# Weight tiles with even and odd columns in separate halves, read one element in turn from each

## The chip, the core and the metric

The kernel runs on one core of one Trainium2 chip. The metric is the device time of one execution in microseconds; lower is better. A core has five engines that run side by side and meet at semaphores: TensorE (PE in the profile, with PEld for its loads of the stationary operand), VectorE (DVE), ScalarE (ACT), GpSimd (POOL) and SyncE (SP), which here issues the transfers of the weights from HBM. A matmul on TensorE holds a stationary operand of 128 x 128 and streams a moving operand of up to 512 columns past it; the result collects in PSUM.

## What is computed

One block of a hybrid layer, for 256 tokens and a model width of 4096, in float32. The parts that matter here are the large products with weights:

```python
h = _rmsnorm(x, norm_w[layer])
u = h @ w_in[layer]                  # 4096 x 15424 columns, split into 16 parts
...
y_ml = hm.reshape(B, S, ML_WIDTH) * jax.nn.sigmoid(ml_o) * jax.nn.silu(ml_z)
y_ns = _nsa(ns_q, ns_kc, ns_vc, ns_ks, ns_vs, ns_kw, ns_vw, ns_g, ...)
```

After these the two halves, the latter gated by silu(ns_z), are joined and multiplied by w_out (4096 x 4096), the input is added, and the sum goes through a last gate: a sigmoid of its product with ple_gate (4096 x 4096), times the product of p with ple_proj (256 x 4096), added to it. Between the products lie a chunked mLSTM, a compression of keys and values, and attention over 256 tokens; their own matmuls are small and have nothing to do with the change.

## The kernel before

**Precision.** Each float32 operand of a large product is held as two parts of the type fp32r, hi and lo, with hi + lo equal to the value up to rounding. A product of x and w is made of three matmuls: x_hi w_hi, x_lo w_hi, x_hi w_lo. The parts of the activations are the tiles sh and sl (and cb for sums and differences of blocks), 128 columns at a time as the stationary operand. The parts of the weights are the tiles whi and wlo; they are the moving operand.

**A unit of weights.** The weights are laid out on the host in blocks of 256 rows by 512 columns, or, for the groups with pairs, 128 rows by two blocks of 512 columns. Either way one unit is a tile of 128 partitions x 2 x 512 float32: 4096 bytes in each partition, the first block (j = 0) in the first 2048 and the second (j = 1) after it. `_blocks` makes this layout for w_in and ple_proj, `_pairs` for the gates, the early groups, w_out and ple_gate.

**The way of a unit.** `load` (L1391) issues its transfer on SP's queue into a raw tile, of which there are six; the first unit is loaded in two parts, one for each block (L1400). `split` (L1427) runs three units ahead of the product: ScalarE copies raw to whi, rounding it (L1416), and VectorE subtracts, wlo = raw - whi (L1417), both over the whole tile of 1024 elements a partition. There are four tiles of whi and of wlo. Then the unit's `mm` issues its matmuls, twelve of 512 columns for a full unit.

**Two kinds of groups.** In a wide group (`wide_group`, L869 and L871) sixteen units with 256 rows each are multiplied with both halves of the tokens. In a pair group (`pair_group`) a plan says, for each pair of row blocks kp, whether it is multiplied plainly ("C": `c_unit`) or by a scheme with seven products in place of eight ("a" and "c": `a_units`, `c_units`), which needs sums of weight blocks. Those sums are VectorE's, in place on raw tiles (`sums`, L1213 to L1217), and of one of its units only the second block is split (`split_one`, L1423 and L1424). Nearly all matmuls of pair groups are issued by `emit`, so their line is L1135 whatever called it; the last unit of the last group is issued in halves of 256 columns at L1248. The products with ple_proj are at L1310 to L1312.

**Order.** The order of the work is written out by hand: the loop at L1469 goes through the units, splits three ahead, issues the loads for which there is a free raw tile, and after each unit lets the smaller tasks (attention, mLSTM, evacuations) take a step.

**Other matmuls.** Units of kind "narrow" (L955, L956) use the split weights as the stationary operand, units of kind "raw" (L976) multiply with the raw tile; the change touches neither. VectorE's additions at L281 (compressed keys and values into xq, with steps of 120 elements in the output) and at L484 (biasc read in steps of 16 elements) are named in the prediction.

Of the kernel before, what the change touches and what calls it, by code (L numbers as in the profile page):

```python
# [13 lines left out]
AF = mybir.ActivationFunctionType  # L14
# [24 lines left out]
XN = (16, 19, 22, 25)  # L39
RAWB = 6  # L40
HALVES = slice(0, 256), slice(256, 512)

# [39 lines left out]
def hymba_block(ctx: ExitStack, tc: tile.TileContext, a, out: bass.AP):  # L84
    nc = tc.nc
# [764 lines left out]
    def wide_group(name, w, stat_flag, post, marks=None):  # L850

        flag = f"ev_{name}"
        box = {}
        prev = evq[-2] if len(evq) >= 2 else None
        evq.append(flag)

        def start():
            if prev:
                require(prev)
            box["ps"] = [psp.tile([128, 512], F32, tag=f"mm{t}", name=f"mm{t}", bufs=2) for t in range(2)]  # L860

        for u in range(16):
            def mm(hi, lo, u=u):
                for j in range(2):
                    c, k = divmod(2 * u + j, 4)
                    first, last = (u == 0 and j == 0), (u == 15 and j == 1)
                    for s, m, st in ((sh, hi, first), (sl, hi, False)):
                        for t in range(2):
                            MM(box["ps"][t], s[c][:, k, t * 128:(t + 1) * 128], m[:, j, :], start=st, stop=False)  # L869
                    for t in range(2):  # L870
                        MM(box["ps"][t], sh[c][:, k, t * 128:(t + 1) * 128], lo[:, j, :], start=False, stop=last)  # L871

            def pre(u=u):
                if u == 0:
                    start()
                if stat_flag and u % 2 == 0:
                    require(f"{stat_flag}{u // 2}")

            def fin(u=u):
                if marks and u % 2:  # L880
                    done.add(f"{marks}{u // 2}")
                if u == 15:
                    post(box["ps"], flag)

            gemm_unit(w[u], mm, pre, fin)
# [252 lines left out]
    def pair_group(g, w, stat):  # L1138
# [70 lines left out]
        def sums(kp, k):  # L1209

            r0, r = raw[kp]
            if k == 0:
                nc.vector.tensor_add(r0[:, 1], r0[:, 1], r0[:, 0])  # L1213
                nc.vector.tensor_add(r0[:, 0], r0[:, 0], r[:, 0])
            else:
                nc.vector.tensor_add(r[:, 0], r[:, 0], r0[:, 1])
                nc.vector.tensor_add(r[:, 1], r[:, 1], r[:, 0])  # L1217

        opened = deque()

# [7 lines left out]
        def c_unit(kp, k, last):  # L1228
            split = split_and_sum

            def mm(hi, lo):
                bl = blocks(kp)
                if last:

                    tail.append((bl, k, hi, lo))
                    if len(tail) < 4:
                        return
                    order = [(t, j) for j in range(2) for t in range(2)]
                    seq = [(b, i) for b in order[0:2] for i in range(3)] + [(b, 3) for b in order[0:2]]
                    for (t, j), i in seq + [(order[2], i) for i in range(4)]:  # L1240
                        bl, k_, hi, lo = tail[i]
                        emit(product(own[t][j], bl(k_, t), hi[:, j], lo[:, j]))
                    t, j = order[3]
                    for c in HALVES:
                        for i in range(4):
                            bl, k_, hi, lo = tail[i]
                            for s, m in ((0, hi), (1, hi), (0, lo)):
                                MM(own[t][j].t[:, c], bl(k_, t)[s], m[:, j, c], start=False, stop=i == 3 and m is lo and c is HALVES[1])  # L1248
                    return
                for j in range(2):  # L1250
                    both(*(product(own[t][j], bl(k, t), hi[:, j], lo[:, j]) for t in range(2)))

            def post():
                if k:
                    finish(kp)
            unit(w[kp, k], split, mm, kp, post=post)

        def a_units(kp):
            def split1(r):
                raw[kp] = [r]  # L1260
                return split_one(r)

            def split2(r):
                raw[kp].append(r)
                opened.extend(((kp, 0), (kp, 1)))
                return split_all(r, keep=True)

            def mm1(hi, lo):
                emit(product(oth[0], blocks(kp)(0, 0), hi[:, 0], lo[:, 0]))

            def mm2(hi, lo):
                both(product(own[0][0], mixed(kp, 2), hi[:, 0], lo[:, 0]),
                     product(own[0][1], blocks(kp)(1, 0), hi[:, 1], lo[:, 1]))
            unit(w[kp, 0], split1, mm1, kp, True)
            unit(w[kp, 1], split2, mm2, kp, True)

        def c_units(kp, last):
            def mm1(hi, lo):
                both(product(oth[3], mixed(kp, 1), hi[:, 0], lo[:, 0]),
                     product(oth[1], mixed(kp, 3), hi[:, 1], lo[:, 1]))  # L1280

            def mm2(hi, lo):
                both(product(oth[2], mixed(kp, 0), hi[:, 0], lo[:, 0]),
                     product(own[1][1], blocks(kp)(1, 1), hi[:, 1], lo[:, 1]))

            def post():
                finish(kp)
                if last:
                    urgent.append(t_x1_oth(g, oth) if 0 <= g < 4 else t_out_oth(g, oth, us))
                    if g in (-1, 3):  # L1290
                        new_activations(g, range(2), 0)
            unit(None, lambda _: split_and_sum(raw[kp][0], kp), mm1)
            unit(None, lambda _: split_and_sum(raw[kp][1], kp), mm2, post=post)

        def p_unit(j):
            box = {}

            def pre():
                require("p")
                require(f"own{g - 1}")  # L1300
                if g == 4:
                    require("r7")
                box["ps"] = [bank(1 - bset, 2 * j + t, [128, 512]) for t in range(2)]

            def mm(hi, lo):
                ps, ph, pl = box["ps"], held["ph"], held["pl"]
                for t in range(2):
                    tk = slice(t * 128, (t + 1) * 128)
                    for k in range(2):
                        MM(ps[t], ph[:, k, tk], hi[:, k, :], start=(k == 0), stop=False)  # L1310
                        MM(ps[t], pl[:, k, tk], hi[:, k, :], start=False, stop=False)
                        MM(ps[t], ph[:, k, tk], lo[:, k, :], start=False, stop=(k == 1))  # L1312

            def t_pj():
                if j == 0:
                    pj[0] = wk.tile([128, 2, 2, 512], F32, tag="a", name="pj")
                for t in range(2):
                    nc.scalar.activation(pj[0][:, j, t], box["ps"][t], AF.Copy)
                if j == 1:
                    done.add(f"pj{g}")  # L1320
                yield
            units.append(dict(src=a["ple_proj"][2 * (g - 4) + 1 - j], mm=mm, pre=pre, post=lambda: urgent.append(t_pj()),
                              kind="pair", split=lambda r: split_all(r)))
# [67 lines left out]
    def load(n):  # L1391
# [5 lines left out]
        raws[n] = wk.tile([128, 8, 64] if units[n]["kind"] == "narrow" else [128, 2, 512], F32, tag="raw", name="raw", bufs=RAWB)  # L1397
        if n == 0:
            for j in range(2):
                nc.sync.dma_start(raws[n][:, j], units[n]["src"][:, j])  # L1400
        else:
            nc.sync.dma_start(raws[n], units[n]["src"])
        if n in XN:
# [16 lines left out]

    def split_one(r):
        hi, lo = split_tiles()
        nc.scalar.activation(hi[:, 0], r[:, 1], AF.Copy)  # L1423
        nc.vector.tensor_sub(lo[:, 0], r[:, 1], hi[:, 0])  # L1424
        return hi, lo

    def split(n):  # L1427
        r = raws.pop(n, None)
        if n == 0:
            hi, lo = split_tiles()  # L1430
            for j in range(2):
                split_x(j)
                nc.scalar.activation(hi[:, j], r[:, j], AF.Copy)
                nc.vector.tensor_sub(lo[:, j], r[:, j], hi[:, j])
            splits[n] = (hi, lo)
            held_raw[0] -= 1
            return
# [69 lines left out]
def _blocks(w, cols):  # L1507

    k = w.shape[0]
    o = np.empty((len(cols), k // 256, 128, 2, 512), w.dtype)  # L1510
    for g, c in enumerate(cols):
        b = w[:, c:c + 512]
        o[g] = b.reshape(k // 256, 2, 128, 512).transpose(0, 2, 1, 3)
    return o


def _pairs(w):

    return np.ascontiguousarray(w.reshape(16, 2, 128, -1, 2, 512)[:, :, :, :, ::-1].transpose(3, 0, 1, 2, 4, 5))


def _layout(i):
# [50 lines left out]
```

## Time and profile before

| what | value |
|---|---|
| median of 3 runs | 2118.67 us (2118.36 to 2118.94) |
| span of the profiled execution, first to last instruction | 2116.5 us |
| what the median has over that span | 2.2 us |
| matmuls, all forms | 9696 |
| moved by the DMA engines | 422.08 MB, 199 GB/s on average |
| whole-tile splits, ScalarE L1416 | 839, mean 1060 ns |
| whole-tile splits, VectorE L1417 | 839, mean 1222 ns |

The time of the profiled execution by itself is not listed apart from the runs; its span is the time from its first to its last instruction. In the profile a row of a group has: line, engine, operation, output<-inputs by the program's names (for a matmul the moving operand comes first), the shape, the count, and after the bar the busy time in us, the mean duration of one in ns, and the idle time of the engine just before them with what ended it. A row of the timeline has the start in us, the duration in us, and the instruction. A row of windows has the stretch, its length, the busy time and count of PE, PEld, DVE, ACT and POOL, the granted clock of TensorE, the busy share of the DMA engines and GB/s. Records of matmuls overlap, since the next one starts while the last one's results are still on their way.

### The profile page before, as it was taken

What the parts mean: (1) busy time and instruction counts of PE and PEld (TensorE: products, weight loads), DVE (VectorE), ACT (ScalarE), POOL (GpSimd) and SP (SyncE); (2) the same over time, 40 slices, a digit from 0 to 9 for tenths busy, and PEclk for the clock granted to TensorE, in tenths of its full rate; (3) what the DMA queues carried; (4) which work ended last, traced back from release to release, by engine and by line L of the source; (5) the groups of instructions that cost most, each with busy time, mean ns of one, the idle gap of its engine ahead of it and who ended that gap; (6) DMA issues with size and microseconds to landing.
All of it is one profiled execution on the core that took longest, in us unless ns stands there. A gap on an engine that the chain in (4) does not pass through costs nothing.

```text
span 2116.5 us, 26925 instructions
## 1 busy us (share of the span) xinstructions
PE 2107.0 (100%) x9696; PEld 1739.3 (82%) x9696; DVE 1679.7 (79%) x2130; ACT 1198.6 (57%) x1545; POOL 30.3 (1%) x69
## 2 busy tenths in 40 slices
PE   9999999999999999999999999999999999999998
PEld 7888788888888888888888888888888888888887
DVE  6697588666656675859989999988898987888988
ACT  6656455555556555456555565666555555555554
POOL 1000000000000000000000000000000000000000
PEclk9999999999999999999999999999999999999999
DMA  9656866654455455646666667565666665666664
GB/s 354 211 185 206 285 203 216 195 167 159 145 174 159 151 177 168 196 145 200 200 206 209 192 207 229 182 213 180 224 211 216 229 221 169 204 201 224 203 218 145
DMA packets 118374, 422.08 MB, mean 199 GB/s; under 512 B 13714, under 2 KB 14026, under 8 KB 118240
## 3 DMA queue, kind: packets, MB, share of 16 engines
q1 hardware_dynamic: 115568, 413.45, 60.4%
q0 software_dynamic: 2528, 6.89, 1.1%
q8 instruction: 76, 1.25, 0.2%
q14 instruction: 58, 0.48, 0.1%
q10 hardware_dynamic: 144, 0.02, 0.0%
HBM read 416.08 MB, written 4.23 MB: 199 GB/s over the span
## 4 chain that ended last, share of the span: by engine, by line
PE 99%; DMA 0%; DVE 0%; ACT 0%; SPq 0%; issue 0%
PE mm L1135 34%; PE sd L1135 33%; PE mm L869 16%; PE mm L871 8%; PE sd L569 1%; PE sd L976 1%; PE sd L558 1%; PE sd L253 0%; PE sd L773 0%; PE sd L582 0%; PE sd L475 0%; DMA raw<-in_w_in 0%; PE sd L525 0%; PE sd L524 0%; PE sd L523 0%; PE mm L956 0%
## 5 line engine op out<-in xcount | busy, mean ns | idle before, releaser
L1416 ACT ACTIVATE whi<-raw 128x1024 fp32r<-128x1024 f32 x839 | 885.1, 1060 | 732.5 <-PE mm L869 133.8
L1417 DVE TENSOR_TENSOR wlo<-raw,whi 128x1024 fp32r<-128x1024 f32 x839 | 1021.9, 1222 | 343.1 <-ACT whi L1416 327.1
L1135 PE MATMUL sd<-whi,sh 128*128 128x512 f32 x852 | 276.1, 390 | 0.0
L1135 PE MATMUL sd<-wlo,sh 128*128 128x512 f32 x852 | 275.7, 389 | 0.0
L1135 PE MATMUL sd<-whi,sl 128*128 128x512 f32 x852 | 275.6, 389 | 0.0
L1135 PE MATMUL mm<-whi,sh 128*128 128x512 f32 x840 | 272.9, 393 | 0.3 <-ACT mv L200 0.3
L1135 PE MATMUL mm<-whi,sl 128*128 128x512 f32 x840 | 270.0, 389 | 0.0
L1135 PE MATMUL mm<-wlo,sh 128*128 128x512 f32 x840 | 269.9, 389 | 0.0
L869 PE MATMUL mm<-whi,sh 128*128 128x512 f32 x768 | 245.1, 400 | 1.4 <-ACT whi L1416 1.4
L869 PE MATMUL mm<-whi,sl 128*128 128x512 f32 x768 | 237.4, 390 | 0.0
L871 PE MATMUL mm<-wlo,sh 128*128 128x512 f32 x768 | 237.1, 390 | 0.0
L1135 PEld LDWEIGHTS sd<-wlo,sh 128*128 128x128 f32 x852 | 159.9, 188 | 33.2
L1135 PEld LDWEIGHTS sd<-whi,sl 128*128 128x128 f32 x852 | 159.9, 188 | 33.2
L1135 PEld LDWEIGHTS sd<-whi,sh 128*128 128x128 f32 x852 | 159.6, 188 | 33.3 <-issue 0.4
L1135 PEld LDWEIGHTS mm<-whi,sl 128*128 128x128 f32 x840 | 157.7, 188 | 33.1
L1135 PEld LDWEIGHTS mm<-wlo,sh 128*128 128x128 f32 x840 | 157.6, 188 | 33.1 <-DVE wlo L1417 0.2
L1135 PEld LDWEIGHTS mm<-whi,sh 128*128 128x128 f32 x840 | 155.8, 188 | 34.4 <-issue 2.7
L871 PEld LDWEIGHTS mm<-wlo,sh 128*128 128x128 f32 x768 | 144.0, 188 | 31.6 <-DVE wlo L1417 0.8
L869 PEld LDWEIGHTS mm<-whi,sl 128*128 128x128 f32 x768 | 144.2, 188 | 31.0
L869 PEld LDWEIGHTS mm<-whi,sh 128*128 128x128 f32 x768 | 139.6, 189 | 29.1 <-issue 1.9
L1135 PE MATMUL mm<-whi,cb 128*128 128x512 f32 x416 | 134.6, 389 | 0.0
L1135 PE MATMUL sd<-whi,cb 128*128 128x512 f32 x352 | 117.5, 389 | 0.0
(315 smaller groups left out, 1875.2 us busy)
## 6 DMA issues: line engine op xcount, KB each, us to landing
raw<-in_w_gate SPq DMA_DIRECT2D x192, 512.0 KB, 3.6
raw<-in_w_in SPq DMA_DIRECT2D x191, 512.0 KB, 3.5
raw<-in_w_out SPq DMA_DIRECT2D x128, 512.0 KB, 4.0
raw<-in_ple_gate SPq DMA_DIRECT2D x128, 512.0 KB, 3.5
raw<-in_w_early SPq DMA_DIRECT2D x96, 512.0 KB, 3.9
raw<-in_w SPq DMA_DIRECT2D x16, 512.0 KB, 4.3
u<-in_xt SPq DMA_DIRECT2D x16, 256.0 KB, 7.7
xn<-in_x SPq DMA_DIRECT2D x4, 1024.0 KB, 7.1
```

The costliest lines, as they stand in the source:

```text
L558: nc.tensor.transpose(psd[i][:, b, s, :], sb[i][:, b, s * 128:(s + 1) * 128], idn)
L569: MM(o[t][:, h, :], ptb[i][:, b, s, :], v[:, s, b, g * 128:(g + 1) * 128], start=False, stop=(i == 6 + t and b == 1 and s == t))
L869: MM(box["ps"][t], s[c][:, k, t * 128:(t + 1) * 128], m[:, j, :], start=st, stop=False)
L871: MM(box["ps"][t], sh[c][:, k, t * 128:(t + 1) * 128], lo[:, j, :], start=False, stop=last)
L976: MM(o[64 * kv:64 * kv + 60], xq[l // 8][:, l % 8, 60 * kv:60 * kv + 60], raw[:, j, 256 * kv:256 * kv + 256], start=(l == 0), stop=(l == 31))
L1135: MM(acc.t, s, m, start=acc.i == 0, stop=acc.i == acc.n - 1)
L1416: nc.scalar.activation(hi, r, AF.Copy)
L1417: nc.vector.tensor_sub(lo, r, hi)
```

## The change

The weights' layout and every access to it change together; the arithmetic is the same. The host now puts, for each partition, the even columns of both blocks into the first 2048 bytes and the odd columns into the second: in each half, 256 elements of block 0 and then 256 of block 1. Two helpers name the parts: `cols(m, j)` is block j as two runs of 256 elements, and `stream(m, j)` is block j in the order of its columns, with the half as the innermost index, so that successive columns are 512 elements apart, forth and back. Every matmul with whi or wlo as its moving operand uses `stream`; partial splits, the sums and the loads and splits of the first unit use `cols`. Whole-tile splits and loads stay as they are. Columns come out in PSUM in the order as before.

```diff
+def cols(m, j):
+    return m[:, :, 256 * j:256 * j + 256]
+
+def stream(m, j, c=slice(0, 512)):
+    return m[:, :, 256 * j + c.start // 2:256 * j + c.stop // 2].rearrange("p h b -> p b h")
...
-                            MM(box["ps"][t], s[c][:, k, t * 128:(t + 1) * 128], m[:, j, :], start=st, stop=False)
+                            MM(box["ps"][t], s[c][:, k, t * 128:(t + 1) * 128], stream(m, j), start=st, stop=False)
...
-                MM(box["ps"][t], sh[c][:, k, t * 128:(t + 1) * 128], lo[:, j, :], start=False, stop=last)
+                MM(box["ps"][t], sh[c][:, k, t * 128:(t + 1) * 128], stream(lo, j), start=False, stop=last)
...
-                nc.vector.tensor_add(r0[:, 1], r0[:, 1], r0[:, 0])
-                nc.vector.tensor_add(r0[:, 0], r0[:, 0], r[:, 0])
+                nc.vector.tensor_add(cols(r0, 1), cols(r0, 1), cols(r0, 0))
+                nc.vector.tensor_add(cols(r0, 0), cols(r0, 0), cols(r, 0))
...
-                    both(*(product(own[t][j], bl(k, t), hi[:, j], lo[:, j]) for t in range(2)))
+                    both(*(product(own[t][j], bl(k, t), stream(hi, j), stream(lo, j)) for t in range(2)))
...
-                nc.sync.dma_start(raws[n][:, j], units[n]["src"][:, j])
+                nc.sync.dma_start(cols(raws[n], j), cols(units[n]["src"], j))
...
-        nc.scalar.activation(hi[:, 0], r[:, 1], AF.Copy)
-        nc.vector.tensor_sub(lo[:, 0], r[:, 1], hi[:, 0])
+        nc.scalar.activation(cols(hi, 0), cols(r, 1), AF.Copy)
+        nc.vector.tensor_sub(cols(lo, 0), cols(r, 1), cols(hi, 0))
...
-        o[g] = b.reshape(k // 256, 2, 128, 512).transpose(0, 2, 1, 3)
+        o[g] = b.reshape(k // 256, 2, 128, 256, 2).transpose(0, 2, 4, 1, 3).reshape(k // 256, 128, 2, 512)
...
-    return np.ascontiguousarray(w.reshape(16, 2, 128, -1, 2, 512)[:, :, :, :, ::-1].transpose(3, 0, 1, 2, 4, 5))
+    v = w.reshape(16, 2, 128, -1, 2, 256, 2)[:, :, :, :, ::-1].transpose(3, 0, 1, 2, 6, 4, 5)
+    return np.ascontiguousarray(v).reshape(-1, 16, 2, 128, 2, 512)
```

The remaining hunks do the same to the other products of the pair groups, to the halves at L1248, to the products with ple_proj and to the split of the first unit.

More of the change, by code (lines that the diff above doesn't have):

```diff
@@ L1212, in sums @@
             if k == 0:
-                nc.vector.tensor_add(r0[:, 1], r0[:, 1], r0[:, 0])
-                nc.vector.tensor_add(r0[:, 0], r0[:, 0], r[:, 0])
-            else:
-                nc.vector.tensor_add(r[:, 0], r[:, 0], r0[:, 1])
-                nc.vector.tensor_add(r[:, 1], r[:, 1], r[:, 0])
+                nc.vector.tensor_add(cols(r0, 1), cols(r0, 1), cols(r0, 0))
+                nc.vector.tensor_add(cols(r0, 0), cols(r0, 0), cols(r, 0))
+            else:
+                nc.vector.tensor_add(cols(r, 0), cols(r, 0), cols(r0, 1))
+                nc.vector.tensor_add(cols(r, 1), cols(r, 1), cols(r, 0))
         opened = deque()
@@ L1241, in mm @@
                         bl, k_, hi, lo = tail[i]
-                        emit(product(own[t][j], bl(k_, t), hi[:, j], lo[:, j]))
+                        emit(product(own[t][j], bl(k_, t), stream(hi, j), stream(lo, j)))
                     t, j = order[3]
@@ L1247, in mm @@
                             for s, m in ((0, hi), (1, hi), (0, lo)):
-                                MM(own[t][j].t[:, c], bl(k_, t)[s], m[:, j, c], start=False, stop=i == 3 and m is lo and c is HALVES[1])
+                                MM(own[t][j].t[:, c], bl(k_, t)[s], stream(m, j, c), start=False, stop=i == 3 and m is lo and c is HALVES[1])
                     return
                 for j in range(2):
-                    both(*(product(own[t][j], bl(k, t), hi[:, j], lo[:, j]) for t in range(2)))
+                    both(*(product(own[t][j], bl(k, t), stream(hi, j), stream(lo, j)) for t in range(2)))
             def post():
@@ L1268, in mm1 @@
             def mm1(hi, lo):
-                emit(product(oth[0], blocks(kp)(0, 0), hi[:, 0], lo[:, 0]))
+                emit(product(oth[0], blocks(kp)(0, 0), stream(hi, 0), stream(lo, 0)))
             def mm2(hi, lo):
-                both(product(own[0][0], mixed(kp, 2), hi[:, 0], lo[:, 0]),
-                     product(own[0][1], blocks(kp)(1, 0), hi[:, 1], lo[:, 1]))
+                both(product(own[0][0], mixed(kp, 2), stream(hi, 0), stream(lo, 0)),
+                     product(own[0][1], blocks(kp)(1, 0), stream(hi, 1), stream(lo, 1)))
             unit(w[kp, 0], split1, mm1, kp, True)
@@ L1278, in mm1 @@
             def mm1(hi, lo):
-                both(product(oth[3], mixed(kp, 1), hi[:, 0], lo[:, 0]),
-                     product(oth[1], mixed(kp, 3), hi[:, 1], lo[:, 1]))
+                both(product(oth[3], mixed(kp, 1), stream(hi, 0), stream(lo, 0)),
+                     product(oth[1], mixed(kp, 3), stream(hi, 1), stream(lo, 1)))
             def mm2(hi, lo):
-                both(product(oth[2], mixed(kp, 0), hi[:, 0], lo[:, 0]),
-                     product(own[1][1], blocks(kp)(1, 1), hi[:, 1], lo[:, 1]))
+                both(product(oth[2], mixed(kp, 0), stream(hi, 0), stream(lo, 0)),
+                     product(own[1][1], blocks(kp)(1, 1), stream(hi, 1), stream(lo, 1)))
             def post():
@@ L1309, in mm @@
                     for k in range(2):
-                        MM(ps[t], ph[:, k, tk], hi[:, k, :], start=(k == 0), stop=False)
-                        MM(ps[t], pl[:, k, tk], hi[:, k, :], start=False, stop=False)
-                        MM(ps[t], ph[:, k, tk], lo[:, k, :], start=False, stop=(k == 1))
+                        MM(ps[t], ph[:, k, tk], stream(hi, k), start=(k == 0), stop=False)
+                        MM(ps[t], pl[:, k, tk], stream(hi, k), start=False, stop=False)
+                        MM(ps[t], ph[:, k, tk], stream(lo, k), start=False, stop=(k == 1))
             def t_pj():
@@ L1432, in split @@
                 split_x(j)
-                nc.scalar.activation(hi[:, j], r[:, j], AF.Copy)
-                nc.vector.tensor_sub(lo[:, j], r[:, j], hi[:, j])
+                nc.scalar.activation(cols(hi, j), cols(r, j), AF.Copy)
+                nc.vector.tensor_sub(cols(lo, j), cols(r, j), cols(hi, j))
             splits[n] = (hi, lo)
```

## The prediction

> **What bounds the kernel now.** I read the page's busy shares first, then the chain that ended last, then the groups of instructions with their shapes kept apart, and last the timeline of TensorE near the end.
>
> ```profile
> span 2116.5 us, 26925 instructions
> ...
> PE 2107.0 (100%) x9696; PEld 1739.3 (82%) x9696; DVE 1679.7 (79%) x2130; ACT 1198.6 (57%) x1545; POOL 30.3 (1%) x69
> ...
> PEclk9999999999999999999999999999999999999999
> ...
> PE 99%; DMA 0%; DVE 0%; ACT 0%; SPq 0%; issue 0%
> PE mm L1135 34%; PE sd L1135 33%; PE mm L869 16%; PE mm L871 8%; PE sd L569 1%; PE sd L976 1%; PE sd L558 1%; PE sd L253 0%; PE sd L773 0%; PE sd L582 0%; PE sd L475 0%; DMA raw<-in_w_in 0%; PE sd L525 0%; PE sd L524 0%; PE sd L523 0%; PE mm L956 0%
> ```
>
> TensorE is at work in 2107.0 of 2116.5 us, at a granted clock in the top tenth throughout, and 99% of the chain that ends last is its own matmuls; the three lines L1135, L869 and L871 are 91% of it. Busy time alone wouldn't prove that TensorE is the limit, since a matmul's record covers more than the time it holds the next one back. So I look at the distance between starts, in the timeline of the last stage: the first and last of 36 matmuls of 512 columns, and the first and last of 24 of 256 columns.
>
> ```profile
> 2098.99 0.39 PE L1135 MATMUL sd<-whi,sh 128*128 128x512 f32 x1
> ...
> 2106.93 0.39 PE L1135 MATMUL sd<-wlo,sh 128*128 128x512 f32 x1
> 2107.15 0.28 PE L1248 MATMUL sd<-whi,sh 128*128 128x256 f32 x1
> ...
> 2109.90 0.28 PE L1248 MATMUL sd<-wlo,sh 128*128 128x256 f32 x1
> ```
>
> The 512-column ones start (2106.93 - 2098.99) / 35 = 0.2269 us apart, the others (2109.90 - 2107.15) / 23 = 0.1196 us. The difference is 107.3 ns for 256 columns: **0.419 ns for a column**, and 226.9 - 512 x 0.419 = 12 ns for a matmul besides. So 95% of a matmul's pace is the streaming of its moving operand, and the change alters just how that operand is read. Whatever it does to a column is paid in full: nothing covers it.
>
> **How many matmuls it touches.** In the groups of TensorE, the moving operand is the first name behind the arrow; every group with whi or wlo there is touched.
>
> ```profile
> L1135 PE MATMUL sd<-whi,sh 128*128 128x512 f32 x852 | 276.1, 390 | 0.0
> L1135 PE MATMUL sd<-wlo,sh 128*128 128x512 f32 x852 | 275.7, 389 | 0.0
> L1135 PE MATMUL sd<-whi,sl 128*128 128x512 f32 x852 | 275.6, 389 | 0.0
> L1135 PE MATMUL mm<-whi,sh 128*128 128x512 f32 x840 | 272.9, 393 | 0.3 <-ACT mv L200 0.3
> L1135 PE MATMUL mm<-whi,sl 128*128 128x512 f32 x840 | 270.0, 389 | 0.0
> L1135 PE MATMUL mm<-wlo,sh 128*128 128x512 f32 x840 | 269.9, 389 | 0.0
> L869 PE MATMUL mm<-whi,sh 128*128 128x512 f32 x768 | 245.1, 400 | 1.4 <-ACT whi L1416 1.4
> L869 PE MATMUL mm<-whi,sl 128*128 128x512 f32 x768 | 237.4, 390 | 0.0
> L871 PE MATMUL mm<-wlo,sh 128*128 128x512 f32 x768 | 237.1, 390 | 0.0
> L1135 PE MATMUL mm<-whi,cb 128*128 128x512 f32 x416 | 134.6, 389 | 0.0
> L1135 PE MATMUL sd<-whi,cb 128*128 128x512 f32 x352 | 117.5, 389 | 0.0
> L1135 PE MATMUL mm<-wlo,cb 128*128 128x512 f32 x208 | 72.0, 390 | 0.0
> L1135 PE MATMUL sd<-wlo,cb 128*128 128x512 f32 x176 | 62.3, 391 | 0.0
> ...
> L1310 PE MATMUL sd<-whi,ph 128*128 128x512 f32 x16 | 6.2, 389 | 0.0
> ...
> L1312 PE MATMUL mm<-wlo,ph 128*128 128x512 f32 x16 | 6.2, 389 | 0.0
> ...
> L1248 PE MATMUL sd<-whi,sl 128*128 128x256 f32 x8 | 2.3, 283 | 0.0
> ```
>
> L1135: 3 x 852 + 3 x 840 + 416 + 352 + 208 + 176 = 6228. L869 and L871: 3 x 768 = 2304. L1310 to L1312: six groups of 16 = 96. Together **8628 of 512 columns**, and 24 of 256 at L1248. They take 8628 x 0.2269 + 24 x 0.1196 = 1961 us, 93% of the span.
>
> **The price of a column read the new way.** Before, a matmul's 512 columns lie in one run of 2048 bytes. After, column 0 is read from the first half of the tile, column 1 from 2048 bytes further on, column 2 from beside column 0, and so on: no column lies beside the one read just before it. No matmul of this trace reads its moving operand so; all read runs (even the two-piece key tiles of L523 to L525 are runs of 128 or more). The nearest rows are VectorE's, where single elements are taken far apart.
>
> ```profile
> L1104 DVE TENSOR_TENSOR y<-y,u 128x1024 f32<-128x1024 f32 x8 | 9.7, 1218 | 0.0
> ...
> L1213 DVE TENSOR_TENSOR raw<-raw 128x512 f32<-128x512 f32 x96 | 65.7, 684 | 0.0
> ...
> L281 DVE TENSOR_TENSOR xq<-ct,pe_c 128x480 f32<-128x480 f32 x8 | 8.5, 1067 | 0.0
> ...
> L484 DVE TENSOR_TENSOR sc<-sd,biasc 128x60 f32<-128x60 f32 x8 | 1.7, 250 | 1.4 <-POOL sc L481 1.4
> ...
> L500 DVE TENSOR_TENSOR sc<-sc,mask_c 128x60 f32<-128x60 f32 x8 | 1.4, 219 | 0.1
> ```
>
> Over runs, VectorE pays (1218 - 684) / 512 = 1.04 ns for an element and 150 ns for the instruction. L281 writes each element 480 bytes from the one before and comes back beside an old one only after eight: (1067 - 150) / 480 = 1.91 ns, **1.83 times** the price of a run. L484 reads biasc in steps of 64 bytes and costs 250 ns where L500, as large and over runs, costs 219: 31 / 60 = 0.52 ns more for an element, **1.50 times**. That is one engine's write and one engine's read, at a pace slower than TensorE's, so they bound and don't settle the price. From below I can't exclude nothing at all: TensorE may hold both places open. From above there are two readings of the same rows. As a ratio they give TensorE 1.5 to 1.83 times a column's 0.419 ns. As a time in itself, if it is the memory and not the engine that sets it, they give 1.04 + 0.52 = 1.56 to 1.91 ns a column, about four times TensorE's present 0.419.
>
> I choose **twice 0.419 ns**. [...] A column then costs 0.419 ns more: 214.5 ns for a matmul of 512 columns, 107.3 for one of 256.
>
> [...]
>
> **The sum.** 8628 x 214.5 ns = 1850.7 us, 24 x 107.3 ns = 2.6 us: +1853 us. Against it stands a little idle time that slower matmuls fill: the 1.4 us at L869 waiting for whi at the start. The profiled span becomes 2116.5 + 1853 - 1.4 = 3968 us; the median of the runs is 2118.67, 2.2 us over that span, for what lies around it. **Forecast 3970 us.** The weight loads (PEld, 82%) run beside the matmuls and are not changed; a load has more time than before.
>
> **The other edits** cost nothing in this forecast. The full splits at L1416 and L1417 still run over the whole tile. The partial split (L1423, L1424) and the sums (L1213 to L1217) now go over two runs of 1024 bytes instead of one of 2048. They stand on VectorE, and what hides them is TensorE; where cover is thinnest is the mixed stage:
>
> ```profile
> 1005.70:1012.50 6.80, 6.80 (x32) 5.63 (x31) 6.69 (x8) 3.00 (x4) 0.00 (x0) 1.00 0.61 189
> ...
> L753 DVE TENSOR_TENSOR s<-s 128x256 f32<-128x256 f32 x13 | 5.5, 425 | 0.5
> ...
> L666 DVE TENSOR_TENSOR s<-mb,future_c 128x256 f32<-128x256 f32 x8 | 3.3, 416 | 0.0
> ```
>
> In that stretch TensorE is busy 6.80 and VectorE 6.69 of 6.80 us. At twice a column's time the same 30 matmuls take about 13.2 us and VectorE's 6.69 are covered twice over. If columns keep their price, the cover is 0.11 us. L753 (two runs) costs 9 ns more than L666 (as many elements), while L1104 shows two longer runs at the price of the plain slope; so 0 to 9 ns each, for 4 x 96 sums and 96 partial splits at most 480 x 9 ns = 4.3 us, if nothing hid it. The first weight load (L1400) keeps its two transfers and its bytes, in pieces half as long; it stands ahead of everything on SP's queue, and I bound its cost by 0 and the 3.5 us that a whole load takes to land.
>
> ```profile
> raw<-in_w_in SPq DMA_DIRECT2D x191, 512.0 KB, 3.5
> ```
>
> No wait is added, and no instruction or byte. What is late next in the forecast is still TensorE: at about 0.44 us a matmul the splits (1.06 and 1.22 us per tile of twelve matmuls) and the loads fall further behind the need for them.
>
> **The rivals.**
>
> *The columns keep their price* (the change then does nothing, whatever the order of the addresses): TensorE's reader fetches ahead and keeps both places open, so each fetch still serves several columns. For it: only two runs are interleaved here, against eight in L281, and the total of bytes touched is the same. Against it: both rows of VectorE show a penalty. Time: 2118.67 plus 0 to 4.3 + 3.5 us, 2119 to 2127, most likely 2119; this is the case that ends on the other side, not slower, and it decides at the point where two open runs are enough. [...] Chance 24%, of which 4% slower by over 0.2%.
>
> *A jump costs the memory's own time.* Each column pays 1.56 to 1.91 ns, as on VectorE. A matmul then takes 512 x 1.56 + 12 = 811 to 512 x 1.91 + 12 = 990 ns, 584 to 763 more: +5039 to +6583 us, 7.2 to 8.7 ms. For it: the penalty on VectorE is a time that no clock of TensorE need shorten. Against it: TensorE already fetches runs at 0.419 ns where VectorE needs 1.04, so its path is not VectorE's. Chance 18%.
>
> *A part of a step.* Some fetches overlap, as by the reading row's 1.50: 0.21 ns x 512 = 107 ns, +926 us, 3045 us; the case spans 2130 to 3600. Chance 10%.
>
> *The jump helps.* If the 12 ns beside the columns came from reads that collide with the writes of the next tile, alternating halves could remove up to 12 x 8652 ns = 104 us: 2015 us. Nothing shows that: the 12 ns are the same for both sizes above and hardly vary. Chance 2%.
>
> **How the numbers follow.** The forecast (a column twice as dear) has 46%, and its own range goes from 1.83 times a column (178 ns more, +1536, 3655 us) to a whole matmul doubled (226.9 ns more, +1958, 4077 us). 0.2% of this kernel, 4.2 us, is about what a measurement can tell. Faster: 2%. Within 0.2%: 24 - 4 = 20%. Slower: 46 + 18 + 10 + 4 = 78%. The range must reach from the unchanged case to the forecast's upper end to hold 24 + 10 + 46 = 80%; the fourfold case and the gain are left out: 2115 to 4080. It is wide since its two main cases lie far apart, with little between.
>
> **What would show it.** Right: in the changed profile the 512-column matmuls of L1135 and L869 start 0.44 us apart, L1248's 0.227; the untouched ones (L569, L523, L955) keep their durations; VectorE's and ScalarE's busy times stay near 1680 and 1199 us, at shares of some 42% and 30%; TensorE stays at 99% of the chain and at full granted clock. Wrong: starts 0.227 us apart (columns keep their price), 0.8 to 1.0 us (the memory's own time), or a lower granted clock, which no step here provides for. L1213 or L1424 longer by more than 9 ns would break the sentence on the other edits.

## The result: faster by 4%, where twice the time was forecast

The changed kernel takes 2035.29 us (median of 4 runs, 2032.81 to 2036.74) against 2118.6 us before (median of 4, 2118.36 to 2118.94). The ratio is 0.9605, with a 95% interval of 0.9592 to 0.9619. The forecast was 3970 us, with a range from 2115 to 4080: the sign was wrong, and the time lies below the range.

The page of the profile after, beside the lines shown of before (L1143 was L1135, L877 and L879 were L869 and L871, L1256 was L1248):

```profile
span 2032.8 us, 26925 instructions
...
PE 2014.3 (99%) x9696; PEld 1748.9 (86%) x9696; DVE 1671.9 (82%) x2130; ACT 1190.7 (59%) x1545; POOL 30.3 (1%) x69
...
PEclk9999999999999999999999999999999999999999
...
PE 90%; DVE 5%; ACT 3%; issue 2%; DMA 1%; SPq 0%; ACTq 0%; DVEq 0%
...
L1143 PE MATMUL sd<-whi,sh 128*128 128x512 f32 x852 | 267.2, 380 | 0.0
...
L1143 PE MATMUL mm<-wlo,sh 128*128 128x512 f32 x840 | 261.3, 379 | 0.9 <-DVE wlo L1425 0.5
...
L877 PE MATMUL mm<-whi,sl 128*128 128x512 f32 x768 | 228.4, 379 | 0.0
```

The same instructions, as many matmuls, the same clock; the touched matmuls of 512 columns last some 10 ns less, 379 in place of 389 in most groups. The timeline of the last stage, the same 36 and 24 matmuls as in the prediction:

```profile
2015.83 0.38 PE L1143 MATMUL sd<-whi,sh 128*128 128x512 f32 x1
...
2023.38 0.38 PE L1143 MATMUL sd<-wlo,sh 128*128 128x512 f32 x1
2023.60 0.27 PE L1256 MATMUL sd<-whi,sh 128*128 128x256 f32 x1
...
2026.17 0.28 PE L1256 MATMUL sd<-wlo,sh 128*128 128x256 f32 x1
```

Matmuls of 512 columns now start (2023.38 - 2015.83) / 35 = **215.7 ns** apart, against 226.9 before; those of 256 columns (2026.17 - 2023.60) / 23 = 111.7 ns, against 119.6. Taken for all of them, that gives 8628 x 11.2 + 24 x 7.9 ns = 96.8 us, an estimate of the gain. The span became 83.7 us shorter, so some 13 us were given back. Idle time of TensorE accounts for 9.0 of them (2116.5 - 2107.0 = 9.5 us before, 2032.8 - 2014.3 = 18.5 after); where the other 4 went was not followed. The chain shows the idle time too: TensorE's share fell from 99% to 90%, with 5% VectorE and 3% ScalarE. In the list of waits (who waited for whom: us in total, times, longest), these rows of TensorE are new:

```profile
PE sd L566 <- ACT s L549: 3.3, 6, 0.6
PE sd L1143 <- DVE wlo L1425: 2.8, 5, 0.9
PE mm L1143 <- DVE wlo L1425: 1.4, 3, 0.5
```

The list of before has no row of TensorE for either supplier. 3.3 us are waits in the attention, six between 470 and 719 us, for tiles that ScalarE writes; 4.2 us are waits for wlo, eight between 933 and 1570 us. In the mixed stage 30 matmuls took 6.80 us before, of which VectorE was busy 6.69; at 215.7 ns they want 6.47 us, which is less than VectorE needs. That does not make VectorE the limit of the whole stage. In this stretch of the changed kernel VectorE is as busy, 6.70 of 7.00 us, and TensorE is never idle:

```profile
1005.00:1012.00 7.00, 7.00 (x34) 6.14 (x33) 6.70 (x8) 3.77 (x5) 0.00 (x0) 1.00 0.71 213
```

A TensorE that is 5% faster (215.7 ns where it was 226.9) runs into its suppliers now and then, no more.

### The profile page after: what moved, and what is told of

The parts are those of the page before. It is cut to its first block, busy times and chain, and to the rows that moved or that the text cites. A ratio compares the mean times of both kernels' runs of the same rounds, so it can differ in the third digit from the quotient of the medians.

```text
span 2032.8 us, 26925 instructions
## 1 busy us (share of the span) xinstructions
PE 2014.3 (99%) x9696; PEld 1748.9 (86%) x9696; DVE 1671.9 (82%) x2130; ACT 1190.7 (59%) x1545; POOL 30.3 (1%) x69
## 3 DMA queue, kind: packets, MB, share of 16 engines
q8 instruction: 76, 1.25, 0.2%
## 4 chain that ended last, share of the span: by engine, by line
PE 90%; DVE 5%; ACT 3%; issue 2%; DMA 1%; SPq 0%; ACTq 0%; DVEq 0%
PE sd L1143 32%; PE mm L1143 32%; PE mm L877 13%; PE mm L879 7%; DVE wlo L1425 2%; ACT whi L1424 2%; ACT s L549 1%; DVE mx L544 1%; DVE s L542 1%; PE sd L984 1%; PE sd L781 1%; PE sd L261 1%; PE sd L577 0%; DMA raw<-in_w_in 0%; PE sd L483 0%
## 5 line engine op out<-in xcount | busy, mean ns | idle before, releaser
L1424 ACT ACTIVATE whi<-raw 128x1024 fp32r<-128x1024 f32 x839 | 879.0, 1055 | 660.1 <-DVE raw L1222 129.1
L1143 PE MATMUL sd<-whi,sh 128*128 128x512 f32 x852 | 267.2, 380 | 0.0
L1143 PE MATMUL sd<-whi,sl 128*128 128x512 f32 x852 | 266.8, 379 | 0.0
L1143 PE MATMUL sd<-wlo,sh 128*128 128x512 f32 x852 | 266.8, 379 | 0.0
L1143 PE MATMUL mm<-whi,sh 128*128 128x512 f32 x840 | 264.1, 383 | 0.6 <-ACT mv L208 0.3
L1143 PE MATMUL mm<-wlo,sh 128*128 128x512 f32 x840 | 261.3, 379 | 0.9 <-DVE wlo L1425 0.5
L1143 PE MATMUL mm<-whi,sl 128*128 128x512 f32 x840 | 261.0, 379 | 0.0
L877 PE MATMUL mm<-whi,sh 128*128 128x512 f32 x768 | 235.9, 389 | 1.6 <-ACT whi L1424 0.8
L879 PE MATMUL mm<-wlo,sh 128*128 128x512 f32 x768 | 228.6, 379 | 0.3
L877 PE MATMUL mm<-whi,sl 128*128 128x512 f32 x768 | 228.4, 379 | 0.0
L1143 PEld LDWEIGHTS sd<-whi,sl 128*128 128x128 f32 x852 | 161.0, 189 | 22.9
L1143 PEld LDWEIGHTS sd<-wlo,sh 128*128 128x128 f32 x852 | 161.0, 189 | 22.8
L1143 PEld LDWEIGHTS sd<-whi,sh 128*128 128x128 f32 x852 | 160.7, 189 | 23.0 <-ACT whi L1424 0.4
L1143 PEld LDWEIGHTS mm<-wlo,sh 128*128 128x128 f32 x840 | 158.4, 189 | 24.6 <-DVE wlo L1425 2.5
L1143 PEld LDWEIGHTS mm<-whi,sh 128*128 128x128 f32 x840 | 156.6, 189 | 25.9 <-issue 2.7
L1143 PEld LDWEIGHTS mm<-whi,sl 128*128 128x128 f32 x840 | 158.8, 189 | 22.5
L879 PEld LDWEIGHTS mm<-wlo,sh 128*128 128x128 f32 x768 | 145.0, 189 | 21.6 <-DVE wlo L1425 1.1
L877 PEld LDWEIGHTS mm<-whi,sl 128*128 128x128 f32 x768 | 145.1, 189 | 20.6
L877 PEld LDWEIGHTS mm<-whi,sh 128*128 128x128 f32 x768 | 140.1, 189 | 21.8 <-issue 1.9
L1143 PE MATMUL mm<-whi,cb 128*128 128x512 f32 x416 | 130.2, 379 | 0.0
L1143 PE MATMUL sd<-whi,cb 128*128 128x512 f32 x352 | 113.8, 379 | 0.0
```

Of the source, the lines that this page charges most:

```text
L877: MM(box["ps"][t], s[c][:, k, t * 128:(t + 1) * 128], stream(m, j), start=st, stop=False)
L879: MM(box["ps"][t], sh[c][:, k, t * 128:(t + 1) * 128], stream(lo, j), start=False, stop=last)
L1143: MM(acc.t, s, m, start=acc.i == 0, stop=acc.i == acc.n - 1)
L1424: nc.scalar.activation(hi, r, AF.Copy)
```

## The experiments

Two questions stood: what makes reading in turn quicker than a run (215.7 ns against 226.9), and what the 11 ns are that a run loses. Unless it is said otherwise, the kernels below are the change with another layout of a block and the matching order of reading; the sums, splits, loads and results are the same. Each was one run with a profile, beside one run of the kernel before (2118.5 to 2119.6 us). The pace is always that of the last 36 matmuls of 512 columns, as above, and two rows of the timeline show it.

**near_1024: in turn, but 1024 bytes apart.**

```diff
-    return m[:, :, 256 * j + c.start // 2:256 * j + c.stop // 2].rearrange("p h b -> p b h")
+    return m[:, j].rearrange("p (h b) -> p b h", h=2)[:, c.start // 2:c.stop // 2]
```

> Columns are read in turn from the two halves of their own block, 1024 bytes apart instead of 2048. Theory A (reading in turn from two places avoids what slows a run, wherever the places are): 512-column matmuls start 215.7 ns apart, time about 2035 us. Theory B (it is the two halves of the 4096-byte tile, a matter of where the places lie): 226.7 ns apart, about 2118 us.

```profile
2015.94 0.38 PE L1143 MATMUL sd<-whi,sh 128*128 128x512 f32 x1
...
2023.50 0.38 PE L1143 MATMUL sd<-wlo,sh 128*128 128x512 f32 x1
```

2034.67 us, 7.56 / 35 = 216.0 ns where the change has 215.7. The halves of the tile have no part in it (B falls).

**step2: no turns, every second place of a run.**

```diff
+    v = m[:, j].rearrange("p (b h) -> p h b", h=2)
+    return v if c.stop - c.start == 512 else v[:, c.start // 256]
```

> A block lies in one run; its even places are read first, then its odd ones, so that each element is 8 bytes from the one before and nothing is read in turn. Theory C (a run of neighbouring elements has a price of its own that any larger step avoids): 215.7 ns apart, about 2035 us. Theory A (only reading in turn helps): 226.7 ns apart, about 2118 us.

```profile
4023.11 0.63 PE L1144 MATMUL sd<-whi,sh 128*128 128x512 f32 x1
...
4038.90 0.63 PE L1144 MATMUL sd<-wlo,sh 128*128 128x512 f32 x1
```

4053.16 us and 451 ns: neither of the two that were expected. A step of 8 bytes costs what the prediction feared of 2048 bytes forth and back. So an order apart from neighbours can have a price (451 ns against 226.9), and the change, at 215.7, does not pay it.

**two_runs: a pattern with two dimensions, but runs.**

```diff
+    if c.stop - c.start == 256:
+        return m[:, c.start // 256, 256 * j:256 * j + 256]
+    return m[:, :, 256 * j:256 * j + 256]
```

> Columns 0 to 255 lie in the first half of the tile and 256 to 511 in the second; a product reads two runs of 256. Theory A and theory C: both see runs, so 226.7 ns apart or a little more for the second run, 2118 to 2130 us. Theory D (a pattern with two dimensions is handled otherwise than one with one): 215.7 ns, about 2035 us.

```profile
2100.85 0.39 PE L1145 MATMUL sd<-whi,sh 128*128 128x512 f32 x1
...
2108.79 0.39 PE L1145 MATMUL sd<-wlo,sh 128*128 128x512 f32 x1
```

2120.15 us, 226.9 ns: as before. The form of the pattern is nothing by itself (D falls).

**half_stat: half of the weight load, runs as before.** This is the kernel before with one line changed.

```diff
-            MM(acc.t, s, m, start=acc.i == 0, stop=acc.i == acc.n - 1)
+            n = 64 if 0 < acc.i < acc.n - 1 else 128
+            MM(acc.t[0:n], s[:, 0:n], m, start=acc.i == 0, stop=acc.i == acc.n - 1)
```

> The layout of before; in the pair groups all matmuls of a sum but the first and the last use 64 of the 128 columns of their stationary operand, which leaves out half of the rows of those products. [...] Theory F (a run costs a fixed time at its start, whatever is loaded): 226.7 ns, about 2118 us.

```profile
2117.81 0.39 PE L1136 MATMUL sd<-whi,sh 128*64 128x512 f32 x1
...
2125.86 0.39 PE L1136 MATMUL sd<-wlo,sh 128*128 128x512 f32 x1
```

2137.23 us, 8.05 / 35 = 230 ns: slower than before, and no longer even. In the pair groups of this run nine in ten single distances lie between 224 and 236 ns; before, nine in ten lay at 226 or 227. Among the last 36 they are 0.22 to 0.24 us by the timeline, where before has 0.22 and 0.23. So half of the load does not make a matmul quicker, yet a run's price isn't quite fixed either (against F).

**turn_step2: in turn, and every second place.**

```diff
+    v = m[:, j].rearrange("p (h b q) -> p q b h", h=2, q=2)
+    return v if c.stop - c.start == 512 else v[:, c.start // 256]
```

> As near_1024, but of each half the even places are read first and the odd ones later: successive columns still come from places 1024 bytes apart in turn, while no column is followed, within a few, by its neighbour of 4 bytes away. Theory R (the reader fetches pieces of at least 8 bytes, keeps the last few of them and is quick as long as each serves two columns within a short time): as dear as step2, 450 ns apart at L1143, about 4050 us. Theory K (two columns are read at a time and it only matters that the two lie in different places): 215.7 ns, about 2035 us.

```profile
2099.06 0.39 PE L1144 MATMUL sd<-whi,sh 128*128 128x512 f32 x1
...
2107.00 0.39 PE L1144 MATMUL sd<-wlo,sh 128*128 128x512 f32 x1
```

2118.38 us, 226.9 ns: to the digit the price of a run, though no column is near the one before it. R (450) and K (215.7) both fall.

**four_ways: one column from each of four quarters, 512 bytes apart.**

```diff
+    return m[:, j].rearrange("p (h b) -> p b h", h=4)[:, c.start // 4:c.stop // 4]
```

> A block lies in four quarters of 512 bytes and its columns are read one from each in turn. Theory R: 215.7 ns and 2035 us if the reader keeps four pieces, about 450 ns and 4050 us if it keeps but two. Theory K: 215.7 ns, 2035 us.

```profile
2578.38 0.45 PE L1143 MATMUL sd<-whi,sh 128*128 128x512 f32 x1
...
2588.30 0.45 PE L1143 MATMUL sd<-wlo,sh 128*128 128x512 f32 x1
```

2600.29 us, 283.4 ns: between the two values expected.

**pairs: two columns from one half, two from the other.**

```diff
+    return m[:, :, 256 * j + c.start // 2:256 * j + c.stop // 2].rearrange("p h (b e) -> p b h e", e=2)
```

> As the change, but two neighbouring columns are read from one half and then two from the other. Theory A in its narrow form (each column must come from another place than the one before): 226.7 ns, about 2118 us, since every second step is one within a run. Theory G (what a run loses it loses by staying in one place for long, not by a single step): 215.7 ns, about 2035 us. Theory R as a price for jumps says nothing against either.

```profile
2997.56 0.50 PE L1143 MATMUL sd<-whi,sh 128*128 128x512 f32 x1
...
3009.23 0.50 PE L1143 MATMUL sd<-wlo,sh 128*128 128x512 f32 x1
```

3021.83 us, 333.4 ns: dearer than both kernels. Turning once for two columns took 118 ns more than turning for each (215.7); no theory had that.

**step_stat: another pattern of the weight load.** The kernel before, with the stationary operand of wide groups and plain blocks read in steps of eight.

```diff
+def every8(s, k, t):
+    return s.rearrange("p k t -> p (k t)")[:, 2 * k + t::8]
```

> The layout and the moving operand of before; the stationary operand of wide groups and plain blocks is read in steps of eight elements (32 bytes) over a chunk of 1024 instead of along 128 neighbours, so that other columns of the activations enter those products. Theory E (the weight load and the stream along a run get in each other's way in the memory): another pattern of the load changes the pace of a contiguous stream, to anything but 226.7 ns; if each piece that the load touches costs the stream a step, to 250 ns or more. Theory F (a fixed price at the start of a run): 226.7 ns, about 2118 us.

A group of weight loads before and in this run, busy us and mean ns, then the idle time before them:

```profile
L1135 PEld LDWEIGHTS sd<-whi,sl 128*128 128x128 f32 x852 | 159.9, 188 | 33.2
...
L1139 PEld LDWEIGHTS sd<-whi,sl 128*128 128x128 f32 x852 | 251.0, 328 | 5.1
```

2270.52 us. A load now takes 328 ns where it took 188, and idles 5.1 us before 852 of them where it idled 33: the loads themselves have become the limit. So this run says nothing on E; it shows that a load pays for steps, too.

### A theory from these eight, and eight runs to try it

No trace shows how TensorE reads its operand, so what follows is a rule of counting that was made to fit the paces so far. Theory L: take the even columns of the stream by themselves and the odd ones by themselves, as two halves, and the tile in pieces of 16 bytes, four neighbouring elements. What counts is **how many columns in a row one half takes from a piece**: column n is to be compared with n + 2, not with n + 1. In the change each half takes four (0, 2, 4, 6 of the stream are four neighbours), at 215.7 ns. In a run it takes two (places 0 and 2, then the next piece), and so it does in turn_step2, both at 226.9 ns. In step2 it takes one (places 0, 4, 8; 451 ns), as in four_ways (283.4) and pairs (333.4). The expectations from here on speak of two halves of a reader that keep a piece each; that is a picture of this count, and no run shows it.

**short: in turn within eight places, 16 bytes apart.**

```diff
+    return m[:, j, c].rearrange("p (g h b) -> p g b h", h=2, b=4)
```

> Within each eight neighbouring places of a block the order is 0, 4, 1, 5, 2, 6, 3, 7: columns are read in turn from two places only 16 bytes apart. Theory L, formed from the runs so far (columns are read two at a time by two halves of the reader, one for the even and one for the odd columns of the stream; each keeps the piece of 16 bytes that it read last, and a piece that serves four columns of one half leaves it free half the time, one that serves two leaves it none): each half gets four columns out of each piece, so 215.7 ns apart and 2035 us, as in the change. Theory M (the two places have to be far apart, in different parts of the memory): 226.7 ns or more, 2118 us or more.

```profile
2015.92 0.38 PE L1143 MATMUL sd<-whi,sh 128*128 128x512 f32 x1
...
2023.47 0.38 PE L1143 MATMUL sd<-wlo,sh 128*128 128x512 f32 x1
```

2034.64 us, 215.7 ns: as L says (M falls).

**fours: four neighbours from one half of the tile, four from the other.** The diff is that of pairs with e=4.

> Four neighbouring columns (16 bytes) from one half of the tile, then four from the other, 2048 bytes apart. Theory L: each half of the reader gets two columns out of each piece, as in a run, so 226.7 ns and 2118 us. Theory G (a run loses by staying in one place): 215.7 ns, 2035 us.

```profile
2294.63 0.42 PE L1143 MATMUL sd<-whi,sh 128*128 128x512 f32 x1
...
2303.38 0.41 PE L1143 MATMUL sd<-wlo,sh 128*128 128x512 f32 x1
```

2314.98 us, 250.0 ns, not the 226.7 of L, and farther from G. With two columns a piece, pieces that alternate between far places took 23 ns more here than pieces in sequence (226.9). L lacks that.

**tiny_stat: an eighth of the weight load, runs as before.** The diff is that of half_stat with 16.

> As half_stat, but with 16 columns of the stationary operand in place of 64, which leaves out seven eighths of the rows of those products; moving operands are runs, as before. Theory E (what a run loses is lost to the weight load read beside it, here an eighth as long): near the 215.7 ns of the change, 216 to 219 ns at L1136, some 60 us less than before. Theory F (a fixed price at the start of a run, whatever is loaded): 226.7 ns, 2118 us.

```profile
L1136 PEld LDWEIGHTS sd<-whi,sl 128*16 128x16 f32 x852 | 80.5, 95 | 113.6
...
2120.93 0.39 PE L1136 MATMUL sd<-whi,sh 128*16 128x512 f32 x1
...
2129.02 0.39 PE L1136 MATMUL sd<-wlo,sh 128*128 128x512 f32 x1
```

2140.4 us, 231.1 ns. A load reads an eighth of the columns and lasts 95 ns in place of 188, and the run pays as much as ever: E, by which the price goes with what the load reads, falls.

**half_stat_turn: half of the weight load, read in turn.** The changed kernel with the diff of half_stat.

> The changed kernel with 64 of 128 columns of the stationary operand in the pair groups, which leaves out half of the rows of those products. In half_stat the pace of runs wavered between 224 and 236 ns. Theory E with L (a reader that is free half the time gives way to the weight load without loss): 215.7 ns without wavering, about 2035 us. If the wavering were the matmul's own with 64 columns: between 213 and 225 ns, some 25 us more.

```profile
2014.83 0.38 PE L1144 MATMUL sd<-whi,sh 128*64 128x512 f32 x1
...
2022.38 0.38 PE L1144 MATMUL sd<-wlo,sh 128*128 128x512 f32 x1
```

2033.55 us, 215.7 ns, with single distances of 215 to 217: the wavering of half_stat is the run's, not that of a matmul with 64 columns.

**swap: places 0, 2, 1, 3 of each four.**

```diff
+    return m[:, j, c].rearrange("p (g h b) -> p g b h", h=2, b=2)
```

> Within each four neighbouring places the order is 0, 2, 1, 3. No column follows its neighbour, yet of each piece of 16 bytes the even columns of the stream take two in a row and the odd ones two, as in a run. Theory L: the price of a run, 226.7 ns apart, about 2118 us. Theory A (any order in which no column follows its neighbour in the memory is quick, as long as nothing is skipped): 215.7 ns, about 2035 us.

```profile
2099.80 0.39 PE L1143 MATMUL sd<-whi,sh 128*128 128x512 f32 x1
...
2107.73 0.39 PE L1143 MATMUL sd<-wlo,sh 128*128 128x512 f32 x1
```

2119.09 us, 226.6 ns: L's value. A is not tried by it, since half of the steps do lead to a neighbouring place (2 to 1, and 3 to the next 0); four_ways, which skips nothing and has no such step, took 283.4 ns against A. Beside short this is the sharpest pair of the study: the same bytes, the same writers, both orders within eight neighbouring places, and 11 ns between them (226.6 and 215.7).

**four_short: four pieces side by side, one column from each in turn.**

```diff
+    return m[:, j, c].rearrange("p (g h b) -> p g b h", h=4, b=4)
```

> Within each sixteen neighbouring places the order is 0, 4, 8, 12, 1, 5, 9, 13 and so on: four pieces of 16 bytes that lie side by side are read in turn. Theory L: each half of the reader changes its piece with every column, as in four_ways, so 280 ns or more, 2600 us or more. Theory M2 (four_ways and pairs were dear since their places lie 512 to 2048 bytes apart): 215.7 to 226.7 ns, 2035 to 2118 us.

```profile
2453.58 0.43 PE L1143 MATMUL sd<-whi,sh 128*128 128x512 f32 x1
...
2462.97 0.43 PE L1143 MATMUL sd<-wlo,sh 128*128 128x512 f32 x1
```

2474.77 us, 268.3 ns: dear, as L has it and M2 has not, though under the 280 given. With the four places side by side a matmul took only 15 ns less than in four_ways (283.4), where they are 512 bytes apart.

**turn_step4: as turn_step2, with steps of four.** The diff is that of turn_step2 with q=4, and its second line cuts the halves of 256 columns to match.

> As turn_step2, but each half of a block is read in steps of four, so that no piece of 16 bytes serves twice within a few columns; successive columns still come from two places in turn. Theory L: each half of the reader needs a new piece for every column, as in step2, four_ways and pairs: 280 to 455 ns, 2600 to 4060 us. Theory R2 (two open places are what counts, whatever the step): 226.7 ns as turn_step2, 2118 us.

```profile
4022.69 0.63 PE L1144 MATMUL sd<-whi,sh 128*128 128x512 f32 x1
...
4038.48 0.63 PE L1144 MATMUL sd<-wlo,sh 128*128 128x512 f32 x1
```

4052.74 us, 451 ns: the value of step2, as the count of L demands. In step2 two successive columns share a piece and here none do; by the count of each half the two are alike, one column a piece. Within L the runs also set the size of the piece: with 8 bytes turn_step2 and turn_step4 would both have one column a piece, and with 32 bytes short and swap would both have four, while each of these pairs differs (226.9 and 451 ns, 215.7 and 226.6).

**lo_runs: whi in turn, wlo in runs.** The products with wlo go to other columns of the result.

```diff
+def runs(m, j, c=slice(0, 512)):
+    return stream(m, j, c).rearrange("p b h -> p h b")
```

> The change, but the products with wlo read two runs of 256 (so that they go to other columns of the result); the products with whi are read in turn. Theory S (each run loses its 11 ns by itself): two of three matmuls at 215.7 and one at 226.7 ns, 219.4 on average, 2035 + 2876 x 11 ns = about 2067 us. Theory Q (a reader that has no time to spare can't make good a small delay at the change of matmuls, and one that has can, ahead of and behind the runs): less than half of the 11 ns is left, 2050 us or less.

```profile
1039.98 0.59 PE L1147 MATMUL sd<-whi,sh 128*128 128x512 f32 x2
1040.41 0.59 PE L1147 MATMUL sd<-whi,sl 128*128 128x512 f32 x2
1040.85 0.63 PE L1147 MATMUL sd<-wlo,sh 128*128 128x512 f32 x2
1041.31 0.59 PE L1147 MATMUL sd<-whi,sh 128*128 128x512 f32 x2
1041.74 0.59 PE L1147 MATMUL sd<-whi,sl 128*128 128x512 f32 x2
1042.17 0.63 PE L1147 MATMUL sd<-wlo,sh 128*128 128x512 f32 x2
1042.64 1.02 PE L1147 MATMUL mm<-whi,cb 128*128 128x512 f32 x4
```

2074.87 us, 8 us over what S gives, and much nearer to S than to Q. The four matmuls in turn take (1040.85 - 1039.98 + 1042.17 - 1041.31) / 8 = 216 ns each, the two runs (1041.31 - 1040.85 + 1042.64 - 1042.17) / 4 = 232 ns. Nothing is made good by the neighbours: a run pays its price in its own time, here rather 16 ns than 11.

All orders of reading together, by the columns that one half of the stream takes from a piece before the next:

| columns a piece | kernels | ns from start to start |
|---|---|---|
| 4 | the change, near_1024, short | 215.7 to 216.0 |
| 2, each half's pieces in sequence | before, two_runs, swap, turn_step2 | 226.6 to 226.9 |
| 2, each half's pieces far apart in turn | fours | 250.0 |
| 1, coming back to the piece soon | four_short, four_ways, pairs | 268.3, 283.4, 333.4 |
| 1, not coming back to it soon | step2, turn_step4 | 451 |

## Why the prediction was wrong

**What bounds the kernel: right.** TensorE's pace set the time, and most of what the touched matmuls saved came through. The count of 8628 and 24 stands; with 11.2 and 7.9 ns it gives 96.8 us, of which 83.7 arrived.

**The price of a column: wrong, and it is the step that failed.** "I choose twice 0.419 ns" was the author's estimate, above the 1.50 to 1.83 times of VectorE's rows. No run shows the 0.419 ns that it adds to each column of the change; a matmul of 512 columns took 11.2 ns less in its place. The choice rested on the sentence that no column lies beside the one read just before it. near_1024, turn_step2 and turn_step4 have that property as well, at 216.0, 226.9 and 451 ns, so it does not set the price. What puts all the runs in order is L's count, which looks at the column two places earlier in the stream. By that measure the change is gentler than a run, four columns to a piece and not two. The rows of VectorE (L281, L484) were of another engine, and in patterns that bring no more than one element from a place before the next; their cousins here are four_ways and step2, which did cost 1.25 and 2 times a run. The size foreseen was right for step2 (451 ns; the forecast's own working gives 226.9 + 214.5 = 441): right for a change that wasn't made. Nor is once or twice all there is: fours, four_short, four_ways and pairs took 1.10, 1.18, 1.25 and 1.47 times a run.

**The 12 ns beside the columns: taken as given, and part of the gain was there.** The prediction worked them out (226.9 - 512 x 0.419) and left them standing as a cost of any matmul. The same working after gives (215.7 - 111.7) / 256 = 0.406 ns for a column and 215.7 - 512 x 0.406 = 8 ns besides. By it, of the 11.2 ns that a matmul of 512 columns saved, between 4 and 5 came off what stands beside the columns and the rest off the columns. Nor could the prediction say that "the 12 ns are the same for both sizes": two sizes give one slope and one constant, and nothing is left over to test them with.

**The rivals.** "The jump helps" had 2% and 2015 us, and was nearest in time. Its mechanism, reads of runs that collide with the writes of the next tile, is not borne out. short and swap have the same writes in the same places and differ by the whole 11 ns; that alone leaves it open that only the one has time to give way to a write. The trace of before settles more. From 199.30 to 201.50 us neither VectorE nor ScalarE nor GpSimd runs, and from 2099 to 2107 us the DMA engines move nothing:

```profile
199.30:201.50 2.20, 2.20 (x12) 1.81 (x11) 0.00 (x0) 0.00 (x0) 0.00 (x0) 1.00 0.76 238
2099.00:2107.00 8.00, 8.00 (x37) 6.64 (x36) 7.12 (x11) 3.23 (x5) 0.00 (x0) 1.00 0.00 0
...
199.40 0.62 PE L1135 MATMUL mm<-whi,sl 128*128 128x512 f32 x2
...
201.21 0.62 PE L1135 MATMUL mm<-wlo,sh 128*128 128x512 f32 x2
```

The eight matmuls of the first stretch start (201.21 - 199.40) / 8 = 226 ns apart, those of the second 226.9: the run's price is the same where the one kind of write is absent and where the other is. "The columns keep their price" was right of turn_step2, two_runs and swap (226.6 to 226.9 ns), but two open places, its reason, are shown by no run, and turn_step4 reads from two in turn at 451 ns. "The memory's own time" (811 to 990 ns) was met by no order that was tried; the dearest took 451.

**The other edits: right.** The sums and partial splits over two shorter runs cost the same: the partial split lasted 685 ns at L1424 before and 684 at L1432 after:

```profile
L1432 DVE TENSOR_TENSOR wlo<-raw,whi 128x512 fp32r<-128x512 f32 x96 | 65.7, 684 | 6.5 <-ACT whi L1431 6.5
```

**What is late next: missed for this sign.** The prediction saw that VectorE's cover is 0.11 us in 6.80 in the mixed stage, but followed it only for a slower TensorE or an equal one. With a faster one 4.2 us of waits for wlo appear, and 3.3 us in the attention that it did not look at.

**What stays open.** That the order of reading makes the gain is shown by short beside swap (215.7 and 226.6 ns); L, as the reason, is not. Its count puts all the orders in the right sequence, but it was fitted after the first eight runs and missed fours by 23 ns and the bound for four_short by 12; where the next piece lies has a part that no run isolates. Why a run loses 11 ns to a matmul is not settled. It is not the amount that the weight load reads (231.1 ns with an eighth of it in tiny_stat), nor, as far as those two stretches go, the writes of the next tile, nor the same everywhere (a run takes 224 to 236 ns in half_stat, 232 in lo_runs). A version with VectorE and ScalarE relieved where TensorE now waits was not tried.

## What to carry to other kernels

Where TensorE streams fp32r operands without a pause, work out the distance from start to start, and try another order of reading before taking it as a cost of the matmul. The layout to try here has four neighbouring places (16 bytes) feed columns n, n + 2, n + 4 and n + 6 of the stream, by a permutation within eight elements as in short (215.7 ns); with two neighbouring places, as in swap, a matmul took 226.6. It gave 4% here; the host's work for it is outside the time measured. A step of two along one run (step2) and a step of four in turn (turn_step4) doubled a matmul (451 ns against 226.9), so try an order on the chip before building on it.

## What the runs showed of the hardware that was not expected

- A moving operand of fp32r in a run is not the quickest: 226.9 ns for 512 columns, against 215.7 to 216.0 when neighbours of two places are read one element in turn, at distances of 16, 1024 and 2048 bytes alike.
- The order 0, 2, 1, 3 is as good as a run to 0.3 ns (226.6), while two columns from each of two places in turn cost 333.4 ns.
- The stationary operand pays for steps as well: a load of 128 columns in steps of 32 bytes lasted 328 ns where one of neighbours lasted 188, and the matmuls beside it slowed down with it (2270.52 us in all).
- With 64 or 16 columns in the stationary operand a stream of runs was slower and uneven, 230 and 231 ns on average where it was 226.9, with single distances of 0.22 to 0.24 us in both.
